# 110 series of products of zeros ahead of the first stage of a hybrid decoder layer

## The chip, the cores and the metric

The kernel runs on one core of a Trainium2 chip. Five engines work side by side, each with a queue of its own that it takes in order: TensorE (PE in the profile, with PEld for the loading of its stationary operand), VectorE (DVE), ScalarE (ACT), GpSimd (POOL) and SyncE (SP), which here only issues DMAs. The metric is the time of one execution on the device in microseconds.

## What is computed

One inference step of one layer, for a prompt of 512 tokens and a sample group of 8 x 8 tokens that share the weights (576 tokens together, width 1024). The layer has three parts, each between two RMS norms:

```python
u = _rms(x) * g_pre_mix
proj = u @ w_in                       # z, xbc, dt, q, k, v, gates, og
...
mix = jnp.concatenate([y_ssd, h_ml], axis=-1) @ w_out
x = x + _rms(mix) * g_post_mix
u = _rms(x) * g_pre_x
qx = (u @ w_xq).reshape(bsz, length, X_HEADS, X_HEAD_DIM)
...
x = x + _rms(o) * g_post_x
u = _rms(x) * g_pre_ffn
f = (jax.nn.silu(u @ w_gate) * (u @ w_up)) @ w_down
x = x + _rms(f) * g_post_ffn
```

The first part mixes a state space scan and an mLSTM scan, the second is attention to a memory of 256 rows, the third a SwiGLU of width 2816. The states and the memory's keys and values are outputs as well.

## The kernel before

The activations lie transposed: 128 features on the partitions, eight feature tiles k, and the 576 tokens in the free dimension. A large product of a weight tile and the tokens is made in fp32r, a reduced form of fp32. To keep the accuracy, both sides are split into a high part and the rest, and three products are summed in one PSUM bank: high weight by high activation, high weight by low activation, low weight by high activation. I call these three a block; a block belongs to one 128 x 128 weight tile and one range of tokens. The helper `gemm` (L200 to L212) does that:

```python
mm(ps, wh, ah, start=i == 0, stop=False)                       # L208
mm(ps, wh, al, start=False, stop=False)                        # L209
m = mm(ps, tiles[order[c]][1], xh(order[c], t0, n), ...)       # L211
```

Each `mm` loads its 128 x 128 stationary operand and streams the moving one. The tokens are cut in two ways: in halves of 256 and 320 (`HALVES`), or of 288 and 288 (`EHALVES`). Eight feature tiles make 24 products in a row for one output tile and one half. The gate, up and down projections run the same three products in `mul` (L1857 to L1859) with 288 columns. The values of the mLSTM (L823) turn the sides round: 128 tokens are the stationary operand, 512 columns of weights move. The memory's values (L803 to L805) do it with 256 columns.

A weight tile arrives as `raw` by a DMA from SyncE's queue; ScalarE casts its high part `whi`, and VectorE subtracts for the low part `wlo` (`split_w`, L177 to L194; in some, GpSimd makes the low part with an adding DMA). These buffers are rings: two `raw`, three `whi`, three `wlo`. Activations and other large things live in slabs of 4608 columns, taken with `SL(slot, ...)`; slot 1 first holds `qk` (L478), whose first write comes after the first tiles of the projection.

PSUM has eight banks. `GP` hands out a ring of three, `MP` another ring of three.

The order of the work: where nothing else is said, the framework's planner puts each engine's instructions into an order, by a simulated time of its own (`schedule_with_timeline_sim`). `tc.issue_after` adds an edge, `tc.high_priority` shifts a part, and `tc.manual_schedule` keeps the written order on the engines named.

The start, around the change: VectorE clears a small tile `wz` (L306), and TensorE multiplies it with itself 21 times into `ps_warm`, a bank of `MP` that nothing reads (L307 to L309). Beside that the parameters, the tokens `xraw` and the first two weight tiles come in (L310 to L339); per feature tile ScalarE makes the high part `uh` and VectorE the low part `ul` of the tokens (L330, L331), and both split the weights. The first products (L347 to L349) follow feature tile by feature tile as these arrive. ScalarE and VectorE sum the squares of the tokens (L274, L275), TensorE sums them over the partitions (L234), and the first stage goes on with `in_tile`, the convolution's tiles (`cb`, L459 to L461) and the gates (`la`, L439).

Of the kernel before, what the change touches and what calls it, by code (L numbers as in the profile page):

```python
# [11 lines left out]
F32 = mybir.dt.float32  # L12
F32R = mybir.dt.float32r
# [6 lines left out]
P = 128  # L20
# [95 lines left out]
def build(nc, tc, ctx, I, O):  # L116
    V, A, G, S, TE = nc.vector, nc.scalar, nc.gpsimd, nc.sync, nc.tensor
    mm = TE.matmul
# [12 lines left out]
    def SL(slot, name, dt=F32, shape=(P, KT, T)):  # L131

        return big.tile(list(shape), dt, name=name, tag="s%d" % slot, bufs=1)
# [5 lines left out]
    def MP(name="m"):  # L139
        return pa.tile([P, 512], F32, name=name, tag="a")  # L140
# [60 lines left out]
    def gemm(ps, units, xh, xl, t0, n, k0=0, k1=None, order=None, late=0):  # L201


        tiles = [(hi[:, j * P:(j + 1) * P], lo[:, j * P:(j + 1) * P]) for hi, lo, nk in units for j in range(nk)]
        order = order or range(len(tiles))
        for i, k in list(enumerate(order))[k0:k1]:
            (wh, wl), ah, al = tiles[k], xh(k, t0, n), xl(k, t0, n)
            mm(ps, wh, ah, start=i == 0, stop=False)  # L208
            mm(ps, wh, al, start=False, stop=False)  # L209
            for c in range(late) if i == late - 1 else [i] if i >= late else ():  # L210
                m = mm(ps, tiles[order[c]][1], xh(order[c], t0, n), start=False, stop=c == len(tiles) - 1)  # L211
        return m  # L212
# [94 lines left out]
    psw = MP("ps_warm")  # L307
    for _ in range(NWARM):
        mm(psw[:, 0:256], wz[:, 0:128], wz, start=True, stop=True, skip_group_check=True)  # L309
    S.dma_start(par, I["par"])  # L310

    wl = [wp.tile([P, 1024], F32R, name="wlo", tag="wlo", bufs=3) for _ in range(2)]
# [3 lines left out]
    for k in range(KT):  # L316
        if k % 2 == 0:
            c = slice(128 * k, 128 * k + 256)
# [42 lines left out]
    stop = gemm(ps0[2][1], [(*w2, KT)], U, UL, 256, 320, 0, NSS)  # L361
# [12 lines left out]
    stop = gemm(ps0[3][0], [(*w3, KT)], U, UL, 0, 256)  # L374
# [343 lines left out]
    for g in range(2):  # L718
        psb = BP("ps_ls")
        pb3 = psb.rearrange("p (h t) -> p h t", h=8)  # L720
        for h in range(8):
            mm(psb[:, h * TS:(h + 1) * TS], sel[:80, 8 * g + h:8 * g + h + 1].to_broadcast([80, P]), cumst[:, TP:T],
               start=h == 0, stop=h == 7, skip_group_check=True)
# [8 lines left out]
        for h in range(8):  # L732
            k, j = h % 2, (8 * g + h) // 2
            mm(psi[64 * k:64 * k + 64, j * TS:(j + 1) * TS], xdts[:, 8 * g + h, :], lm[:, h, :], start=True, stop=True,
               skip_group_check=True)
# [12 lines left out]
    for b in range(4):  # L748
# [3 lines left out]
        for g in range(2):  # L752
            for hb in (1, 0):
# [3 lines left out]
                   start=b == 0, stop=b == 3, skip_group_check=True)  # L757
# [139 lines left out]
    for h in range(4):  # L897
        q, k = qk[:, h, :], qk[:, 4 + h, :]
# [11 lines left out]
        for c in range(4):  # L910
            mm(pss[:, c * P:(c + 1) * P], k[:, c * P:(c + 1) * P], q[:, c * P:(c + 1) * P], start=True, stop=True,
               skip_group_check=True)
# [39 lines left out]
    for h in range(4):  # L952
        mm(psb[:, h * TS:(h + 1) * TS], sel[:68, h:h + 1].to_broadcast([68, P]), sxst[:, TP:T], start=h == 0, stop=h == 3,
           skip_group_check=True)
# [22 lines left out]
    for hb in range(2):  # L977
# [6 lines left out]
        for b in range(4):  # L984
# [3 lines left out]
            for h in range(4):  # L988
                mm(psn[32 * h:32 * h + 32, 0:257], qpad[:, h, bb, :], c0[:, h, 0:257], start=False, stop=b == 3,
                   skip_group_check=True)  # L990
# [242 lines left out]
    x = SL(1, "x1")  # L1233
# [267 lines left out]
    def xo(j, i, pool=None):  # L1501

        t0, n = EHALVES[i]

        with tc.issue_after(evx[j - 3].ins if j > 2 else ovs[5].ins):
            ps, w = GP("ps_xo")[:, :n], weights(("xo", j), I["wxo"][j], pool=pool, cut=1024)

        def step(k0, k1):
            m = gemm(ps, [(*w, KT)], act(oh), act(ol), t0, n, k0, k1, [2, 3, 4, 5, 6, 7, 0, 1], 6 if j == 3 else 0)
            if k1 < KT:  # L1510
                return m
            add_sq(ph, ssq, ps, j if i == 0 else XO1.index(j), n, t0=t0)
            evx.append(A.activation(f[:, j, t0:t0 + n], ps, AF.Copy, scale=PAR("g_postx", j)))
            return m, evx[-1]
        return step
# [10 lines left out]
    for j in range(8):  # L1526
        step = xo(j, 0, wx if 3 < j < 7 else None)
# [21 lines left out]
    W, B = {}, {}  # L1549
# [816 lines left out]
```

## Time and profile before

| | |
|---|---|
| median of the two runs | 1083.56 us (1082.75 to 1084.37) |
| the profiled execution | 1084.31 us |
| its span | 1082.5 us |
| TensorE busy | 1069.4 us, 8124 products recorded |
| VectorE, ScalarE, GpSimd busy | 752.6, 611.0, 226.8 us |
| HBM read and written | 160.28 MB and 20.65 MB |

The span is the time between the first and the last instruction that the profiler recorded. A product's listed duration is not what it costs in a stream: products are pipelined, the next starts before the one before has ended, and the step from start to start is the price. A few per cent of the product records can be missing from a trace. In the timeline a row shows the start, the duration, the engine and line, the operands and the count; in the windows each engine has its busy time and count.

### The profile page before, as it was taken

What the parts mean: (1) busy time and instruction counts of PE and PEld (TensorE: products, weight loads), DVE (VectorE), ACT (ScalarE), POOL (GpSimd) and SP (SyncE); (2) the same over time, 40 slices, a digit from 0 to 9 for tenths busy, and PEclk for the clock granted to TensorE, in tenths of its full rate; (3) what the DMA queues carried; (4) which work ended last, traced back from release to release, by engine and by line L of the source; (5) the groups of instructions that cost most, each with busy time, mean ns of one, the idle gap of its engine ahead of it and who ended that gap; (6) DMA issues with size and microseconds to landing.
All of it is one profiled execution on the core that took longest, in us unless ns stands there. A gap on an engine that the chain in (4) does not pass through costs nothing.

```text
span 1082.5 us, 20708 instructions
## 1 busy us (share of the span) xinstructions
PE 1069.4 (99%) x8124; PEld 1015.6 (94%) x8124; DVE 752.6 (70%) x1507; ACT 611.0 (56%) x1098; POOL 226.8 (21%) x305
## 2 busy tenths in 40 slices
PE   9999999999999999999999999999999999999997
PEld 8999887778999999999999979999999999999997
DVE  6796785748887785558755546766467887787556
ACT  7767532346564556556545545646467566656653
POOL 1342642313122121000144301100011121111000
PEclk9999999999999999999999999999999999999999
DMA  6785635436564439753458775644476687578532
GB/s 207 171 158 121 168 107 190 165 77 189 166 176 124 131 93 331 234 198 103 154 196 291 265 253 185 226 145 96 132 175 143 153 204 168 118 187 187 128 131 89
DMA packets 58966, 182.29 MB, mean 168 GB/s; under 512 B 6604, under 2 KB 11852, under 8 KB 58356
## 3 DMA queue, kind: packets, MB, share of 16 engines
q1 hardware_dynamic: 42740, 138.06, 38.8%
q0 software_dynamic: 15552, 41.95, 19.7%
q8 instruction: 64, 1.05, 0.4%
q10 hardware_dynamic: 576, 0.95, 0.2%
q14 instruction: 34, 0.28, 0.1%
HBM read 160.28 MB, written 20.65 MB: 167 GB/s over the span
## 4 chain that ended last, share of the span: by engine, by line
PE 86%; DVE 5%; ACT 4%; issue 2%; DMA 2%; POOL 0%; DVEq 0%; SPq 0%; ACTq 0%; POOLq 0%
PE ps_in L209 4%; PE ps_in L211 4%; PE ps_in L208 4%; PE ps_v L823 3%; PE ps_o L211 3%; PE ps_g L1858 3%; PE ps_g L1857 3%; PE ps_o L209 3%; PE ps_g L1859 3%; PE ps_o L208 3%; PE ps_u L1858 3%; PE ps_u L1859 3%; PE ps_u L1857 3%; PE ps_dn L1857 2%; PE ps_dn L1858 2%
## 5 line engine op out<-in xcount | busy, mean ns | idle before, releaser
L208 PE MATMUL ps_in<-uh,whi 128*128 128x320 f32 (+1 forms) x544 | 162.5, 299 | 1.5 <-DVE cb L459 0.8
L186 ACT CAST whi<-raw 128x1024 fp32r<-128x1024 f32 (+1 forms) x104 | 105.3, 1014 | 101.3 <-PE ps_in L209 24.7
L211 PE MATMUL ps_in<-uh,wlo 128*128 128x320 f32 (+1 forms) x544 | 162.1, 298 | 0.4 <-DMA wlo<-win 0.4
L209 PE MATMUL ps_in<-ul,whi 128*128 128x320 f32 (+1 forms) x544 | 161.4, 297 | 0.0
L193 DVE TENSOR_TENSOR wlo<-raw,whi 128x512 fp32r<-128x512 f32 (+1 forms) x96 | 94.1, 982 | 77.9 <-ACT whi L186 76.7
L208 PEld LDWEIGHTS ps_in<-uh,whi 128*128 128x128 f32 x544 | 102.3, 188 | 4.8 <-issue 2.3
L211 PEld LDWEIGHTS ps_in<-uh,wlo 128*128 128x128 f32 x544 | 102.3, 188 | 1.6 <-DMA wlo<-win 0.6
L209 PEld LDWEIGHTS ps_in<-ul,whi 128*128 128x128 f32 x544 | 102.4, 188 | 0.6
L191 POOL DMA_DIRECT2D wlo<-win x32 | 27.8, 870 | 80.0 <-ACT wlo L190 72.0
L1857 PE MATMUL ps_g<-b,whi 128*128 128x288 f32 x144 | 42.5, 295 | 0.0
L1858 PE MATMUL ps_g<-b,whi 128*128 128x288 f32 x144 | 42.4, 295 | 0.0
L1858 PE MATMUL ps_u<-b,whi 128*128 128x288 f32 x144 | 42.3, 294 | 0.0
L1857 PE MATMUL ps_u<-b,whi 128*128 128x288 f32 x144 | 42.2, 294 | 0.0
L1830 ACT CAST whi<-rawx 128x1024 fp32r<-128x1024 f32 (+1 forms) x26 | 25.6, 987 | 27.6 <-PE ps_dn L1858 13.7
L198 DVE TENSOR_TENSOR wlo<-sw,whi 128x1024 fp32r<-128x1024 f32 (+1 forms) x26 | 29.6, 1140 | 15.0 <-ACT whi L197 14.9
L208 PE MATMUL ps_xo<-qh,whi 128*128 128x288 f32 x128 | 38.4, 302 | 0.2 <-ACT whi L186 0.2
L209 PE MATMUL ps_xo<-ql,whi 128*128 128x288 f32 x128 | 37.8, 296 | 0.0
L211 PE MATMUL ps_o<-mixm_h,wlo 128*128 128x256 f32 (+1 forms) x128 | 37.7, 295 | 0.0
L209 PE MATMUL ps_o<-mixm_l,whi 128*128 128x256 f32 (+1 forms) x128 | 37.5, 293 | 0.0
L211 PE MATMUL ps_xq<-u2h,wlo 128*128 128x320 f32 (+1 forms) x128 | 37.5, 294 | 0.0
L1809 ACT CAST whi<-raw 128x1024 fp32r<-128x1024 f32 (+1 forms) x26 | 25.6, 984 | 21.1 <-PE ps_g L1858 9.5
L211 PE MATMUL ps_o<-mixs_h,wlo 128*128 128x320 f32 (+1 forms) x128 | 37.5, 293 | 0.0
(769 smaller groups left out, 3847.6 us busy)
## 6 DMA issues: line engine op xcount, KB each, us to landing
raw<-win SPq DMA_DIRECT2D x35, 512.0 KB, 4.1
raw<-wout SPq DMA_DIRECT2D x17, 512.0 KB, 3.8
raw<-wxq SPq DMA_DIRECT2D x13, 512.0 KB, 5.6
raw<-wgate SPq DMA_DIRECT2D x13, 512.0 KB, 3.6
raw<-wup SPq DMA_DIRECT2D x13, 512.0 KB, 5.1
wlo<-win POOLq DMA_DIRECT2D x24, 256.0 KB, 5.2
kva<-vc SPq DMA_DIRECT2D x11, 512.0 KB, 4.9
raw<-wv SPq DMA_DIRECT2D x10, 512.0 KB, 3.9
```

Of the source, the lines that this page charges most:

```text
L186: casts.append(A.copy(hi[:, :n], raw[:, :n]))
L191: G.dma_start(lo[:, a:b], src[:, a:b], accum_op=ALU.add)
L193: e.tensor_tensor(lo[:, a:b], raw[:, a:b], hi[:, a:b].bitcast(F32), op=ALU.subtract)
L198: (eng or V).tensor_tensor(lo, src, hi.bitcast(F32), op=ALU.subtract)
L208: mm(ps, wh, ah, start=i == 0, stop=False)
L209: mm(ps, wh, al, start=False, stop=False)
L211: m = mm(ps, tiles[order[c]][1], xh(order[c], t0, n), start=False, stop=c == len(tiles) - 1)
L823: mm(ps, a, b, skip_group_check=True, **kw)
L1809: s.c1 = A.copy(s.h1[:, s.all], s.r1[:, s.all])
L1857: mm(ps, wh, b[0][k], start=start and k == 0, stop=False, skip_group_check=True)
L1858: mm(ps, wh, b[1][k], start=False, stop=False, skip_group_check=True)
L1859: m = mm(ps, wl, b[0][k], start=False, stop=k == nk - 1, skip_group_check=True)
```

## The change

Behind the 21 warm-up products, and ahead of everything else on TensorE, stands a series of products of zeros. A slab of 4608 fp32r columns, `bench`, is taken from slot 1 and cleared by VectorE. There are 110 strings of six letters. A, B and C are the three products of one block, a, b and c those of the next block: A and C read the same moving operand, B one that lies 1024 columns further; A and B use the same weights, C weights that lie 480 columns further. The first 36 strings are all orders of ABC followed by all orders of abc, the other 74 mix the two blocks. For each string eight segments are written, 12 products in seven of them and 24 in one, with 320, 256, 288 or 512 moving columns; the blocks of a segment advance by 576 columns (one segment: by 288). In the segment of 512 the sides are turned round. All products of the probe go into one bank of `MP`, `ps_probe`, which nothing reads; the first product of a segment clears it. The probe's order is kept as written on TensorE. Nothing else of the kernel is edited; in the changed file the lines behind it stand 22 further.

```diff
     psw = MP("ps_warm")
     for _ in range(NWARM):
         mm(psw[:, 0:256], wz[:, 0:128], wz, start=True, stop=True, skip_group_check=True)
+
+    bench = SL(1, "bench", F32R, (P, 4608))
+    V.memset(bench.bitcast(F32), 0.0)
+    ORDERS = 'ABCabc ABCacb ABCbac ABCbca ABCcab ABCcba ACBabc ACBacb ACBbac ACBbca ACBcab ACBcba BACabc BACacb BACbac BACbca BACcab BACcba BCAabc BCAacb BCAbac BCAbca BCAcab BCAcba CABabc CABacb CABbac CABbca CABcab CABcba CBAabc CBAacb CBAbac CBAbca CBAcab CBAcba BAacCb bCcABa cAbBaC caCABb bAcBCa bCcaBA aCbBcA caAbCB CAbacB cbABaC BcabCA acBACb bBAcaC CcbABa bBAaCc cbBAaC aCAbBc ABcbCa cbBCAa bCcBAa cAabCB BaAbcC aAbCBc aBCbAc cabCBA bCABac cbABCa CBbAac acbABC AbCcaB AbBcCa CbABca CAcaBb cBbCaA abBcCA AcBaCb AbBacC ABabcC AcbaBC CaAcBb cBbACa ACcabB CabBAc aACcBb BCbaAc CabcBA cCbABa BbcAaC abcACB bBcAaC aBcCbA ABaCcb AcCbBa cCABab cBbaAC ACaBcb ACbBca AbBaCc caBbCA CcbAaB bcaACB bBcCaA CcbaBA AaBbCc BCaAcb aCBAbc acABbC BAcabC CaABbc cAbCBa bBcaAC BbACac BCcAba BacbAC'.split()
+    SEG = []
+    for o in ORDERS:
+        SEG += [(o, 320, 576, 256, 12), (o, 256, 576, 0, 12), (o, 320, 576, 256, 12), (o, 256, 576, 0, 12),
+                (o, 288, 576, 0, 12), (o, 288, 576, 32, 12), (o, 288, 288, 0, 24), (o, 512, 576, 0, 12)]
+    pq = MP("ps_probe")
+    with tc.manual_schedule(engines={TE.engine}):
+        for o, n, step, at0, count in SEG:
+            for i in range(count):
+                c = o[i % 6]
+                k = (i // 6 * 2 + (c > "C")) % (4 if step == 576 else 8)
+                c = c.upper()
+                x = 64 + at0 + step * k + (1024 if c == "B" else 0)
+                w = 3600 + (480 if c == "C" else 0)
+                if n == 512:
+                    mm(pq[:, 0:n], bench[:, x:x + P], bench[:, w:w + n], start=i < 1, stop=True, skip_group_check=True)
+                else:
+                    w += 128 * (k % 4)
+                    mm(pq[:, 0:n], bench[:, w:w + P], bench[:, x:x + n], start=i < 1, stop=True, skip_group_check=True)
     S.dma_start(par, I["par"])
 
     wl = [wp.tile([P, 1024], F32R, name="wlo", tag="wlo", bufs=3) for _ in range(2)]
```

## The prediction

> **What bounds the kernel now.** I read the page first (busy shares, clock, chain), then the windows of the first 100 us, then what TensorE waits for, and last the timeline of TensorE alone in four places.
>
> ```profile
> span 1082.5 us, 20708 instructions
> ...
> PE 1069.4 (99%) x8124; PEld 1015.6 (94%) x8124; DVE 752.6 (70%) x1507; ACT 611.0 (56%) x1098; POOL 226.8 (21%) x305
> ...
> PEclk9999999999999999999999999999999999999999
> ...
> q8 instruction: 64, 1.05, 0.4%
> ...
> q14 instruction: 34, 0.28, 0.1%
> ...
> PE 86%; DVE 5%; ACT 4%; issue 2%; DMA 2%; POOL 0%; DVEq 0%; SPq 0%; ACTq 0%; POOLq 0%
> ```
>
> TensorE (PE) is busy for 1069.4 of 1082.5 us at nearly the full granted clock, and the chain that ended last lies on it for 86%. All its idle time is 13.1 us. Whatever is put on TensorE's queue is therefore paid in full, except what fits into those 13.1 us. The profiled execution took 1084.31 us: 1.8 us more than its span, and 0.75 us more than the median of 1083.56.
>
> The change puts products on TensorE, so its price is a number of products times the step from one product to the next. The busy column can't give that step, because products overlap: a 320-column product is listed with 0.30 us, while the next one starts after half of that. I take the step from start times over whole groups of 24 products (8 blocks of three), first rows of neighbouring groups:
>
> ```profile
> 60.75 0.30 PE L208 MATMUL ps_in<-uh,whi 128*128 128x320 f32 x1
> ...
> 64.24 0.28 PE L208 MATMUL ps_in<-uh,whi 128*128 128x256 f32 x1
> ...
> 66.96 0.30 PE L208 MATMUL ps_in<-uh,whi 128*128 128x320 f32 x1
> ...
> 70.46 0.28 PE L208 MATMUL ps_in<-uh,whi 128*128 128x256 f32 x1
> ```
>
> From 60.75 to 64.24 lie 24 products of 320 columns: 3.49 us, 145.4 ns each. From 66.96 to 70.46 lie 24 more: 3.50 us, 145.8 ns each. I take 145.6 ns. Between them, from 64.24 to 66.96, lie 24 products of 256 columns: 2.72 us, 113.3 ns each.
>
> ```profile
> 826.22 0.30 PE L1857 MATMUL ps_g<-u3h,whi 128*128 128x288 f32 x1
> ...
> 829.38 0.29 PE L1857 MATMUL ps_g<-b,whi 128*128 128x288 f32 x1
> ```
>
> 24 steps of 288 columns lie between these two rows: 3.16 us, 131.7 ns each.
>
> ```profile
> 221.81 0.48 PE L823 MATMUL ps_v<-wlo,uh 128*128 128x512 f32 x1
> 222.12 0.40 PE L823 MATMUL ps_v<-whi,uh 128*128 128x512 f32 x1
> ...
> 225.83 0.40 PE L823 MATMUL ps_v<-whi,ul 128*128 128x512 f32 x1
> ```
>
> From 222.12 to 225.83 there are 16 steps of 512 columns: 3.71 us, 231.9 ns each. Here the activations are the stationary side and the weights move, as in the last segment of the change.
>
> **The change, part by part.** Each of the 110 order strings makes eight segments: 12 products of 320 columns, 12 of 256, again 12 and 12 of these, 12 of 288, 12 of 288 shifted by 32 columns, 24 of 288 at a distance of 288, and 12 of 512. That is 24 + 24 + 48 + 12 = 108 products, and 11,880 in all, each with its own weight load (the page has x8124 loads beside x8124 products).
>
> - **The products.** One order costs 24 x 145.6 = 3494 ns, 24 x 113.3 = 2719 ns, 48 x 131.7 = 6322 ns and 12 x 231.9 = 2783 ns, together 15.318 us. Times 110 that is 1685.0 us. All of it is on the path: the probe stands ahead of the first stage in TensorE's queue, every real product stands behind it in the same queue, and a TensorE that runs 99% of the time has nowhere else to put it.
> - **Their weight loads** cost nothing beside that: the groups above hold one load for each product, and their steps contain what the loads cost.
> - **The orders.** The groups above run in one order, hi·hi, lo·hi, hi·lo, block after block. It is one of the 110; the others are not in the trace, so I bound them from both sides. The cheapest column in the quoted groups is that of the 256 group, 113.3 / 256 = 0.4426 ns. An order has 33,792 columns; all of them at that rate make 14.96 us, and 110 orders 1645 us. The dearest long run of 256 columns is this:
>
> ```profile
> L803 PE MATMUL ps_v<-wmh,memhl x16: 283/283/284, 497.8 to 503.2; 128*128 128x256 f32 x16
> ```
>
> L804 and L805 stand between these 16, so 45 steps fill 5.4 us: 120.0 ns each, 1.059 times 113.3. All widths dearer by that factor make 1785 us. This run has its weights in another slab than the weight rings, so other distances between weights and activations; the probe copies those of the ring (its names A, B and C are the three products of a block, at the offsets of the kernel's own tiles). The reordered products read the same places at the same distances, so I take the value of the nearest rows, 1685.0, and keep both ends for the range.
> - **The clock during 1.7 ms of zeros.** The kernel's own warm-up multiplies zeros too:
>
> ```profile
> L309 PE MATMUL ps_warm<-wz x21: 272/421/422, 1.1 to 4.9; 128*128 128x256 bf16 x21
> ...
> 4.65 0.49 PE L309 MATMUL ps_warm<-wz 128*128 128x256 bf16 x3
> ```
>
> Its last three products are two steps apart in 0.49 - 0.27 us, 0.11 us for a step, and the fp32r groups that follow run at the steps above. So zeros keep the clock granted, and I cost the clock at nothing; at half the clock the probe would take twice as long.
> - **The memset.** 4608 columns of one slab on VectorE, right after the memset of the warm-up's tile:
>
> ```profile
> 0.84 0.17 DVE L306 MEMSET wz<- 128x128 uint32 x1 [0.84 <-PEq L2358]
> ...
> 5.48 0.39 PE L347 MATMUL ps_in<-uh,whi 128*128 128x256 f32 x1 [0.34 <-ACT whi L197]
> ...
> L198 DVE TENSOR_TENSOR wlo<-sw,whi 128x1024 fp32r<-128x1024 f32 x18 | 22.0, 1223 | 14.9 <-ACT whi L197 14.9
> ```
>
> It starts at about 1.0 and takes at least the 0.17 of the small one and at most 4.5 x 1.223 = 5.5 us, so it ends between 1.2 and 6.5. The warm-up ends at 4.65 + 0.49 = 5.14. The probe thus waits 0 to 1.4 us; I take 0.5, a start at 5.6, where the first real product started at 5.48: +0.1 us. What is queued behind the memset on VectorE are the first low halves (`ul`, `wlo`), and only products behind the probe wait for these: 1685 us of cover.
> - **The inputs.** The DMA queues and ScalarE go on during the probe until the rings are full (two `raw`, three `whi`, three `wlo`), so at its end the first tiles lie ready. What that can save is TensorE's early waiting:
>
> ```profile
> 5.00:20.00 15.00, 14.66 (x111) 14.38 (x110) 11.27 (x21) 10.96 (x21) 0.96 (x3) 1.00 0.91 311
> 20.00:40.00 20.00, 18.47 (x140) 17.42 (x139) 15.02 (x29) 13.14 (x20) 5.92 (x19) 1.00 0.43 117
> ...
> PE ps_ss L234 <- DVE ssqx L275: 1.2, 1, 1.2
> ...
> PE ps_in L208 <- DVE cb L459: 0.8, 1, 0.8
> ```
>
> The first windows idle 0.34 and 1.53 us. The sums of squares (1.2 us) need only the inputs and are done during the probe; `cb` is made from TensorE's own results, so its wait and those like it stay. I take 1.2 + 0.3 = 1.5 us off, with 13.1 us (all idle time) as the most that can go. On the dear side the planner, which orders each queue by a simulated time, may now order the first stages otherwise; another 13 us is the bound I set there, the idle time once more.
> - **Instructions.** (1.05 + 0.28) MB for 20,708 instructions is 64 bytes each; 23,760 more make 1.5 MB. TensorE takes one pair in 15.318 / 108 = 142 ns in the probe, and takes one in 131.7 ns in the 288 group without a gap, so I cost the fetch at nothing. The DMA engines, which have little to do once the rings are full, cover it; without that cover the price would be gaps between products.
> - **Places.** The zero slab shares its slot with `qk`, first written long after the probe. The probe's PSUM bank is one of the ring of three; it is free when its last product ends, and TensorE's next users come later in the same queue. Both cost nothing.
>
> Sum, against the profiled execution: 1084.3 + 1685.0 + 0.1 - 1.5 = 2767.9 us, rounded to 2768.
>
> **The rivals.**
> - *The plain stream rate.* The fp32r steps hold more than the columns need, and this part may come from traffic that is absent in the probe or from the kernel's order. For it speaks the warm-up: 0.109 us for 256 columns (0.11 above), 0.426 ns for a column. Against it: in the quoted 256 group the steps stay at 113.3 as an average of 24, and in the 320 and 288 groups at even more a column, in places of quite different load. It would give 33,792 x 0.426 x 110 = 1583 us, so 2666.
>
> The Trainium skill, "TensorE: Matmul & The Clock Gate", section "Back-to-back issue gap", gives a warm gap of N / 2.4 + 2.5 ns. By it an order takes 14.35 us, the probe about 1579 us and the kernel about 2661, as an estimate from that page. This case's trace does not follow it for fp32r: 113.3, 131.7, 145.6 and 231.9 ns stand against 109.2, 122.5, 135.8 and 215.8.
> - *Dear orders.* If mixing two blocks brings the worse distances of L803 into most orders, all products cost 1.059 times as much: 1785 us, so 2867. The 120.0 ns speak for it, the copied distances against it.
> - *Weight loads that show.* If a load can no longer run beside the product ahead of it, the step grows; the step from 221.81 to 222.12 is 0.31 in place of 0.232. At one product in six this is 1980 x 0.08 = 158 us: 2926. Against it: every product has a new load already, and PEld is busy 94% of the span beside PE.
> - *Not slower.* Nothing reads the probe's bank, so something on the way may drop its products, or they may lie in idle time. Then the time stays at 1084. The warm-up's bank is not read either, and its 21 products are all in the row of L309; the idle time holds 13.1 us at most. It decides only if fewer than 150 products remain (2% is 21.7 us, at 142 ns each).
>
> **How the numbers follow.** The forecast has 0.85, the plain rate 0.05, dear orders 0.05, loads that show 0.03, not slower 0.01, and something unforeseen 0.01. The range begins at the cheap end of the forecast, 1084.3 + 1645 - 1.4 = 2728, and ends where half the products are dear, 1685 + 50, so 2818; the 13 us of the planner lie inside. What lies outside has about 0.15. A measurement of this kernel can tell about 2% from no change: slower by more than that 0.985, within it 0.01, faster 0.005.
>
> **What the profile after would show.** Some 20,000 products in place of 8124, 10,560 of them on the added line for 256 to 320 columns and 1,320 on that for 512; a clock of nines throughout; VectorE, ScalarE and DMA nearly empty from about 20 us to 1690 us; then the old picture. The groups' first starts should lie 24 x 0.1456 us and so on apart. A first real product before 1650 or after 1740 us would say that the steps were wrong; a remainder behind the probe longer or shorter than 1077 us by more than 13 us, that the side effects were.

## The result and the profile after

The changed kernel takes 2772.35 us (median of two runs, 2771.82 and 2772.87), against 1083.56 before: 2.5565 times as long, with an interval of 2.5518 to 2.5611. The forecast was 2768. First the page of the changed kernel, the lines that answer to those of before:

```profile
span 2771.1 us, 44473 instructions
...
PE 2758.5 (100%) x20004; PEld 2648.3 (96%) x20004; DVE 755.5 (27%) x1508; ACT 611.3 (22%) x1098; POOL 226.9 (8%) x305
...
PEclk9999999999999999999999999999999999999999
DMA  2000000000000000000000001654647466657773
...
q8 instruction: 156, 2.56, 0.4%
...
PE 95%; DVE 2%; ACT 1%; DMA 1%; issue 1%; POOL 0%; DVEq 0%; ACTq 0%; POOLq 0%; SPq 0%
PE ps_probe L331 50%; PE ps_probe L328 11%; PE ps_in L209 2%; PE ps_in L208 2%; PE ps_in L211 2%; PE ps_v L845 1%; PE ps_o L211 1%; PE ps_g L1880 1%; PE ps_g L1879 1%; PE ps_o L209 1%; PE ps_g L1881 1%; PE ps_o L208 1%; PE ps_u L1880 1%; PE ps_u L1881 1%; PE ps_u L1879 1%
```

Exactly 11,880 products were added, and the other engines' busy times are within 3 us of those before. In 23 of the 40 slices the DMA engines are busy for less than a tenth, while TensorE works on at the full granted clock. The probe's two lines make 61% of the chain. Its edges, and the memset ahead of it, in the timeline:

```profile
1.91 3.90 DVE L312 MEMSET bench<- 128x4608 f32 x1 [0.91 <-issue]
...
5.74 0.69 PE L369 MATMUL ps_in<-uh,whi 128*128 128x256 f32 x3 [0.52 <-ACT whi L197]
6.26 12.69 PE L331 MATMUL ps_probe<-bench 128*128 128x320 f32 x96
...
1693.69 2.94 PE L328 MATMUL ps_probe<-bench 128*128 128x512 f32 x12
1696.47 0.28 PE L370 MATMUL ps_in<-ul,whi 128*128 128x256 f32 x1
```

The probe lasts from 6.26 to 1696.47, 1690.2 us, where the sum had 1685.0. Three real products slipped in ahead of it. What lies around the probe is 2771.1 - 1690.2 = 1080.9 us, against the old span of 1082.5. To see where those 1.6 us came from, the same two products in the kernel before and in the changed one:

```profile
85.08 0.31 PE L211 MATMUL ps_in<-uh,wlo 128*128 128x320 f32 x1
...
1075.09 0.30 PE L2200 MATMUL ps_ft<-c,sw 128*128 128x128 f32 x1
```

```profile
1772.32 0.31 PE L211 MATMUL ps_in<-uh,wlo 128*128 128x320 f32 x1
...
2763.65 0.31 PE L2222 MATMUL ps_ft<-c,sw 128*128 128x128 f32 x1
```

The distance is 1687.24 us at the first pair and 1688.56 at the last. The probe took 1690.2 us and the first product started 0.26 us later than before; less 1687.24 that is 3.2 us won up to the first pair. Behind it 1.3 us are lost again. TensorE's waits in the changed kernel name some of the places:

```profile
PE ps_os L1430 <- DMA kva<-vc: 1.0, 2, 0.7
PE ps_in L208 <- DVE cb L481: 0.8, 1, 0.8
...
PE ps_os L1430 <- ACT kva L1455: 0.4, 1, 0.4
```

The wait of 1.2 us for the sums of squares is gone, the 0.8 for `cb` is still there, and 1.4 us at L1430, for the sample group's cached keys and values, is new.

### The profile page after: what moved, and what is told of

Its sections match the earlier page's. It is cut to its first block, busy times and chain, and to the rows that moved or that the text cites. A ratio compares the mean times of both kernels' runs of the same rounds, so it can differ in the third digit from the quotient of the medians.

```text
span 2771.1 us, 44473 instructions
## 1 busy us (share of the span) xinstructions
PE 2758.5 (100%) x20004; PEld 2648.3 (96%) x20004; DVE 755.5 (27%) x1508; ACT 611.3 (22%) x1098; POOL 226.9 (8%) x305
## 4 chain that ended last, share of the span: by engine, by line
PE 95%; DVE 2%; ACT 1%; DMA 1%; issue 1%; POOL 0%; DVEq 0%; ACTq 0%; POOLq 0%; SPq 0%
PE ps_probe L331 50%; PE ps_probe L328 11%; PE ps_in L209 2%; PE ps_in L208 2%; PE ps_in L211 2%; PE ps_v L845 1%; PE ps_o L211 1%; PE ps_g L1880 1%; PE ps_g L1879 1%; PE ps_o L209 1%; PE ps_g L1881 1%; PE ps_o L208 1%; PE ps_u L1880 1%; PE ps_u L1881 1%; PE ps_u L1879 1%
## 5 line engine op out<-in xcount | busy, mean ns | idle before, releaser
L331 PEld LDWEIGHTS ps_probe<-bench 128*128 128x128 f32 x10560 | 1397.3, 188 | 9.5
L331 PE MATMUL ps_probe<-bench 128*128 128x288 f32 (+2 forms) x10560 | 1403.0, 294 | 0.0
L328 PE MATMUL ps_probe<-bench 128*128 128x512 f32 x1320 | 322.8, 393 | 0.0
L328 PEld LDWEIGHTS ps_probe<-bench 128*128 128x128 f32 x1320 | 241.9, 188 | 47.6
L186 ACT CAST whi<-raw 128x1024 fp32r<-128x1024 f32 (+1 forms) x104 | 105.4, 1014 | 104.9 <-PE ps_in L209 31.4
```

The costliest lines, as they stand in the source:

```text
L186: casts.append(A.copy(hi[:, :n], raw[:, :n]))
L328: mm(pq[:, 0:n], bench[:, x:x + P], bench[:, w:w + n], start=i < 1, stop=True, skip_group_check=True)
L331: mm(pq[:, 0:n], bench[:, w:w + P], bench[:, x:x + n], start=i < 1, stop=True, skip_group_check=True)
```

## The experiments

The steps below are the mean differences of neighbouring start times in the trace, by the width of the first of the two, over all products of the probe (ns). "Rest" is the span less the probe.

| kernel | 256 | 288 | 320 | 512 | probe, us | rest, us |
|---|---|---|---|---|---|---|
| the prediction's rows | 113.3 | 131.7 | 145.6 | 231.9 | 1685.0 | |
| changed kernel | 115.05 | 131.93 | 145.79 | 231.07 | 1690.2 | 1080.9 |
| e1, one order | 114.65 | 131.61 | 145.46 | 231.67 | 1687.4 | 1079.7 |
| e2, dearest order | 118.39 | 132.16 | 146.59 | 231.38 | 1702.8 | 1079.2 |
| e3, bf16 | 109.17 | 122.5 | 135.86 | 215.67 | 1578.4 | 1081.3 |
| e4, dear distance | 119.80 | 132.52 | 146.56 | 229.22 | 1705.5 | 1084.1 |
| e7, data | 115.22 | 131.93 | 146.35 | 231.07 | 1692.2 | 1088.1 |
| e8, one product | 116.04 | 132.64 | 146.59 | 229.17 | 1696.2 | 1088.9 |
| e9, only 256 | 113.34 | | | | 1346.4 | 1081.8 |

In e3 some records of 512 columns are missing, so its 288 is worked out from the total: (1578.4 - 2.640 x 109.17 - 2.640 x 135.86 - 1.320 x 215.67) / 5.280. The steps from one product of 288 columns to the next, which no missing record touches, give 122.50 too. The rest of e7 includes 6.6 us by which its probe starts later.

**e1 and e2: one order alone.**

```diff
-    ORDERS = 'ABCabc ABCacb ...'.split()
+    ORDERS = ['ABCabc'] * 110        # e1
+    ORDERS = ['aAbCBc'] * 110        # e2
```

> All 110 strings are ABCabc, the kernel's own order. Theory (the step belongs to width, operand type and order, and the quoted groups of the kernel are this order): one order takes 15.311 us as its single instance did in the changed kernel, so 1684.2 us of probe in place of 1690.2 and 2766.4 us in all. Rival (the orders' differences in one instance are chance): no difference, 2772.

> All 110 strings are aAbCBc, the dearest order of the changed kernel (15.480 us in its one instance). Theory (the order fixes the step): 1702.8 us of probe, 2785.0 us. Rival (chance): 2772.

Measured: 2772.48 us (2768.91 to 2775.79) and 2786.43 us (2783.75 to 2788.63). These medians are less sharp than the question, since the rest varies (the four executions of e1 alone lie 6.9 us apart); the probe's edges in the timeline, first of e1 and then of e2, settle it.

```profile
6.17 12.74 PE L331 MATMUL ps_probe<-bench 128*128 128x320 f32 x96
...
1693.59 0.28 PE L370 MATMUL ps_in<-ul,whi 128*128 128x256 f32 x1
```

```profile
6.16 12.82 PE L331 MATMUL ps_probe<-bench 128*128 128x320 f32 x96
...
1708.91 0.28 PE L370 MATMUL ps_in<-ul,whi 128*128 128x256 f32 x1
```

The dearest order takes 1702.8 us, as forecast: its differences in one instance were no chance. The kernel's order takes 1687.4 us, between the two expectations. Step by step the reason is seen. These are the steps of the two 256 segments in e1, in ns, the same within 1 ns in all repetitions:

```
behind 320 columns:  117 123 118 115 120 118 114 113 113 114 113 113
behind 320 columns:  113 114 113 113 114 113 113 114 113 113 114 113
```

The same twelve products, at the same addresses, cost 116.0 ns in one segment and 113.3 in the other. Only what ran before differs: the first of them comes behind the 320 segment that follows the 512 one. In this order a step depends on the products before it and settles after some seven. In aAbCBc it does not come down: both 256 segments of e2 hold 118.4 ns.

**e9: only 256 columns.** All strings are ABCabc here too.

```diff
-        SEG += [(o, 320, 576, 256, 12), (o, 256, 576, 0, 12), ...]
+        SEG += [(o, 256, 576, 0, 12)] * 9
```

> All strings ABCabc, and all nine segments of 12 are of 256 columns (108 products, as before). In the one-order run the 256 segment behind one of 320 began at 117 to 123 ns and fell to 113.3 within seven products, the next one stayed at 113.3. Theory (a step depends on what ran before it, and settles): all at 113.33 ns, 1346.4 us of probe and 2428 to 2430 us. Rival (the mean of the mixture, 114.65 ns, is the price of the order): 1362 us of probe, 2444 us.

Measured: 2429.96 us (2429.58 to 2435.94). The timeline's edges:

```profile
6.32 15.27 PE L330 MATMUL ps_probe<-bench 128*128 128x256 f32 x133
...
1352.75 0.28 PE L369 MATMUL ps_in<-ul,whi 128*128 128x256 f32 x1
```

1346.4 us for 11,880 products is 113.3 ns each. With no other width between them the 256 products stay at the settled step, so the 114.65 of e1 belong to the mixture. For this order the theory of a settling step holds.

**e3: bf16.**

```diff
-    bench = SL(1, "bench", F32R, (P, 4608))
-    V.memset(bench.bitcast(F32), 0.0)
+    bench = SL(1, "bench", BF16, (P, 4608))
+    V.memset(bench, 0.0)
```

> The same orders with a bf16 slab of zeros, so that the same column offsets are half as many bytes apart. Theory (the part of the step above the plain stream rate belongs to the 4-byte operands, as the warm-up's 0.109 us for 256 bf16 columns says): about 0.426 ns a column, 1583 us of probe, 2665 us; by the rule of the Trainium skill, TensorE: Matmul & The Clock Gate, section Back-to-back issue gap, an estimate of 1579 us of probe and 2661 us. Rival (it belongs to the orders, to the weight loads or to the traffic beside): 2772.

Measured: 2661.77 us (2660.35 to 2664.29). The edges in the timeline, and the weight loads of the 512 products among the instructions of L328, first of the changed kernel and then of e3:

```profile
6.64 11.98 PE L331 MATMUL ps_probe<-bench 128*128 128x320 bf16 x96
...
1585.01 0.47 PE L370 MATMUL ps_in<-ul,whi 128*128 128x256 f32 x1
```

```profile
L328 PEld LDWEIGHTS ps_probe<-bench x1320: 187/188/192, 18.7 to 1696.0; 128*128 128x128 f32 x189
...
L328 PEld LDWEIGHTS <-bench x1320: 97/98/98, 18.3 to 1584.8; 128*128 128x128 bf16 x189
```

In bf16, with the same orders and columns, the probe takes 1578.4 us. So the plain rate exists, and the 112 us above it belong to the operand type, fp32r in place of bf16, and not to the orders or the traffic beside, which are the same. Whether the four bytes or another trait of fp32r is behind it was not tested. A weight load's record is 98 ns in bf16 and 188 in fp32r; whether the surplus comes from the loads or from the moving operand's reads, this run doesn't part. The distances in bytes were halved as well; the run in which the weights were moved (e4) shows 15 us, not 112.

The Trainium skill's rule for the gap of an isolated product, N / 2.4 + 2.5 ns ("TensorE: Matmul & The Clock Gate", section "Back-to-back issue gap"), meets the bf16 steps of this stream to 0.2 ns at all four widths; on the fp32r steps it is 5.9 to 15.2 ns too low.

**e4: the dear distance.**

```diff
-                w = 3600 + (480 if c == "C" else 0)
+                w = 3520 + (512 if c == "C" else 0)
```

> The weights moved from column 3600 to 3520 and the C weights to 512 columns behind the A weights in place of 480, so that weights and moving operand lie a multiple of 256 bytes apart, as in the memory's values (120.0 ns for 256 columns). Theory (this distance dears the 256 products alone, since the 256 step is near the length of a weight load): 256 columns at about 119.5 ns, the others as before, plus 12 us, 2784 us. Rival (it dears every width by 1.059): about 2870. Rival (distances do nothing): 2772.

Measured: 2787.84 us (2786.79 to 2791.32). The edges:

```profile
6.25 12.93 PE L331 MATMUL ps_probe<-bench 128*128 128x320 f32 x96
...
1711.71 0.28 PE L370 MATMUL ps_in<-ul,whi 128*128 128x256 f32 x1
```

The probe grows by 15.3 us. The 256 products go to 119.80 ns, as in the memory's values, and bring 12.5 of it (2640 x 4.75). That the place of the weights matters is shown; the edit moved their first column and the distance of the C weights together, and which of the two did it is not. That it matters for 256 columns alone was too simple, since 288 and 320 rose by 0.6 and 0.8 ns and 512 fell by 1.9. A factor of 1.059 on every width is excluded. Why 256 suffers most stays open: the expectation's reason, a step near the length of a weight load, isn't what the records show, 188 ns for an fp32r load and 113 to 120 for the step.

**e8: the same product six times.**

```diff
-    ORDERS = 'ABCabc ABCacb ...'.split()
+    ORDERS = ['AAAAAA'] * 110
```

> All strings are AAAAAA: every second block, six times the same moving operand and the same weights in a row. Theory (the step above the bf16 rate belongs to reading 4-byte operands, and the order only shifts it by a per cent): 1670 to 1700 us of probe, 2752 to 2782 us. Rival (it comes from going to another place with each product): the bf16 steps, 1578 us of probe, 2661 us. Rival (a load of the same weights is left out or cheaper): less still in the 256 products, which are near the load's own length.

Measured: 2781.72 us (2779.16 to 2786.89). The edges, and TensorE's longest waits:

```profile
6.29 12.82 PE L331 MATMUL ps_probe<-bench 128*128 128x320 f32 x96
...
1702.48 0.28 PE L370 MATMUL ps_in<-ul,whi 128*128 128x256 f32 x1
```

```profile
PE ps_os L1430 <- ACT kva L1455: 3.3, 1, 3.3
PE ps_os L1430 <- DMA kva<-vc: 1.7, 2, 1.0
PE ps_o L208 <- ACT f_mix L1115: 1.2, 2, 0.9
```

1696.2 us: going to no other place saves nothing, and weights that were just loaded are loaded again at no lower price. The surplus is not the price of moving about. The waits tell another thing: this kernel's instructions stand in the same order on every engine as the changed kernel's, and yet its rest is 8 us longer, mainly in waits for `kva` and `f_mix` that the changed kernel has shorter or not at all. Behind two of the waits for `kva`, the granted clock (the third figure from the right) was halved for 3.4 us:

```profile
2332.40:2335.70 3.30, 3.30 (x13) 1.60 (x12) 0.00 (x0) 0.00 (x0) 0.00 (x0) 0.50 0.94 380
```

The four executions of e8 alone lie 7.7 us apart, and the profiled one is the longest of them. The rest is uncertain by that much. Seven kernels have this same order on every engine: the changed one, e1 to e4, e8 and e9. In all seven the product that started at 85.08 us before comes 2.3 to 3.2 us earlier than 85.08 us and the probe together. What they lose behind it ranges from nothing to 9.3 us. So the early gain repeats, and the later loss does not.

**e7: data in place of zeros.**

```diff
-    V.memset(bench.bitcast(F32), 0.0)
+    S.dma_start(xs, I["xT"])
+    V.tensor_copy(bench.rearrange("p (k t) -> p k t", t=T), xs)
```

> The slab holds the tokens in place of zeros (a DMA into the slab of xs, and a copy by VectorE in place of the memset), so the probe multiplies data. Theory (the step doesn't depend on the values): probe of 1690.2 us, begun some 8 us later because it waits for the DMA and the copy, 2780 us. Rival (zeros are cheap, data lower the clock or lengthen the steps): a longer probe and a granted clock below 0.99.

Measured: 2781.76 us (2780.52 to 2782.53), granted clock 0.999.

```profile
12.22 0.85 PE L370 MATMUL ps_in<-uh,whi 128*128 128x256 f32 x2 [6.50 <-ACT whi L197]
12.87 14.64 PE L332 MATMUL ps_probe<-bench 128*128 128x320 f32 x96
...
1705.02 0.28 PE L371 MATMUL ps_in<-ul,whi 128*128 128x256 f32 x1
```

The probe starts 6.6 us later and takes 1692.2 us, 2 us more, which lie at its beginning: its first row of 96 products takes 14.64 us in place of 12.69, behind a TensorE that had idled for 6.5 us. The first steps, in ns:

```
320 columns:  314 267 266 267 267 266 267 267 266 267 267 266
256 columns:  214 213 213 214 122 116 119 123 118 115 120 118
```

These are steps at half the clock. The trace of e5 below has a granted clock of 0.50 from 80.4 to 83.8 us, and there 320 columns of the kernel's own products take 267 ns too, just behind it 146. The first warm-up products of the changed kernel take 213 ns for 256 columns of bf16. So at half the clock the fp32r surplus isn't there, and a step at half the clock is 1.8 to 1.9 times one at the full clock and not twice. A mean of 0.999 doesn't show such a beginning. These 24 products hold all of the 1.9 us; from the 25th on every step is that of the zeros within 1 ns. The values don't set the step.

**e5 and e6: no products, and a tenth of them.**

```diff
-    for o in ORDERS:
+    for o in ():                     # e5
+    for o in ORDERS[:11]:            # e6
```

> The slab and its memset stay, the 11,880 products go. Theory (all but a microsecond of the change is the products' steps): the memset delays the first real product by 0.26 us as in the changed kernel, so the time of the kernel before plus 0.3. Rival (the slab, the bank or the planner's order cost or save microseconds of their own): off by 2 us or more.

> Only the first 11 of the 110 strings. In the changed kernel these took 169.1 us. Theory (price proportional to the products, and once for all about 1.6 us less for the rest of the kernel, as 2771.1 less 1690.2 of probe stands to 1082.5): the kernel before plus 167.5. Rival (a fixed price at the start or end of the probe, or a rate that sinks in a long probe): more than 3 us off.

Measured: e5 1083.04 us against 1084.22 of the kernel before beside it, a ratio of 0.9983 (0.9972 to 0.9993); e6 1254.5 us, 170.3 above.

```profile
5.91 12.76 PE L331 MATMUL ps_probe<-bench 128*128 128x320 f32 x96
...
175.08 0.28 PE L370 MATMUL ps_in<-ul,whi 128*128 128x256 f32 x1
```

The eleven orders of e6 take 169.2 us, as the first eleven of the 110 did, so the price is proportional; its total is 2.8 us above the expectation, all of it in the rest (1084.1). The median of e5 is 1.2 us below the kernel before, where +0.3 was expected; that is less than the rival's 2 us off. TensorE's list of waits in e5 begins so:

```profile
PE ps_ct L584 <- ACT r L563: 1.2, 1, 1.2
PE ps_warm L309 <- DVE wz L306: 1.1, 1, 1.1
```

The wait of 1.2 us for the sums of squares is gone here as well, with no probe to make time for them; so is that of 0.8 for `cb`. The memset and the slab alone give the planner other simulated times, and it writes another order on TensorE, VectorE, ScalarE, GpSimd and SyncE. The changed kernel's order differs as well, both from that of the kernel before and from that of e5. The product after the sums, first before and then in e5:

```profile
25.85 0.40 PE L208 MATMUL ps_in<-uh,whi 128*128 128x320 f32 x1
```

```profile
24.86 0.39 PE L208 MATMUL ps_in<-uh,whi 128*128 128x320 f32 x1
```

It starts 1.0 us earlier. The product that started at 60.07 us before comes 1.8 us earlier in e5, and 2.3 in the changed kernel, less the probe. So most of this gain needs no probe, and what the inputs that lie ready add to it can't be told apart from the planner's order. At the product that started at 85.08 us before, the profiled execution of e5 has 0.2 us of it left; between the two stand the 1.2 us at L584 and a stretch at half the clock:

```profile
80.00:84.00 4.00, 4.00 (x18) 3.81 (x18) 3.90 (x7) 3.90 (x7) 2.14 (x5) 0.57 0.79 183
```

## Why the prediction was right, point by point

- *The products.* Right to 0.3%: 1690.2 for 1685.0 us. The 5.2 us are the term of the steps: 256 columns 2640 x 1.75 ns = 4.6, 288 columns 5280 x 0.23 = 1.2, 320 columns 0.5, and 512 columns -1.1. The group from which 113.3 was read was a settled one; behind other widths and in other orders the mean step is 113 to 118 ns (e1, e2).
- *The orders.* Bounded rightly. Over the 110 strings an order takes 15.298 to 15.480 us, 1.2% apart, and the kernel's own, at 15.311 in its one instance, is among the cheapest.
- *The weight loads, the clock of zeros, the instructions.* All three at nothing, and so it came: the steps contain the loads (PEld x20004), the granted clock stayed full and data ran at the same steps (e7), and q8 grew by 1.51 MB without a gap. That half the clock would have doubled the probe was a little too much: e7's first steps are 1.8 to 1.9 times the full ones.
- *The memset.* 3.90 us, from 1.91 to 5.81, within its bounds. The probe began at 6.26 and not at 5.6, but three real products used that time; the first of them came 0.26 us late in place of 0.1. That is not the memset's doing: the product waited for `whi`, and in e5, with the same memset, it started at 5.38, 0.1 us earlier than before. No run shows a price of the memset.
- *The inputs.* The size came out by luck, and the reason isn't borne out. 3.2 us went in the first stages where 1.5 were forecast, and 1.3 came back, mostly at L1430; behind the first pair, kernels in the same order lost from nothing (e2) to 9.3 us (e8). The step that isn't borne out is the one that counted on the full rings, since e5 shows most of the early gain without the probe. The planner's order, which the prediction had as a bound of 13 us and not as a term, was at work; how much of the 3.2 us is its share stays open.
- *The rivals.* The plain rate was a true rate of the wrong operand type (e3). Dear orders and a dear place of the weights exist, at 1% of the probe and not at 5.9% (e2, e4). Loads that show, and products that vanish, did not occur.

The profiled execution took 2772.87 us, 5.0 above the sum of 2767.9: 5.2 from the steps, and 0.2 back from the rest (1080.9 - 1082.5 = -1.6, for +0.1 - 1.5).

## What to carry to other kernels

On an engine that is busy all the time, added work costs its count times its step; read the step from start times over a whole group, not from the busy column, and for the same operand type. A group read in one place is a settled one: other orders, neighbours and places moved the whole probe here by 1% and 256 columns alone by up to 6% (113.3 to 119.8 ns). Don't explain microseconds around such a block by readiness before a run without the block has shown that the planner hasn't simply written another order.

## What the runs showed of the hardware

- At the full granted clock, the step of an fp32r product is above that of bf16 at every width: 113.3 to 109.2 ns at 256 columns, 131.9 to 122.5 at 288, 145.8 to 135.9 at 320, 231.1 to 215.7 at 512.
- At half the clock it is not: 213 ns for 256 columns of either type (the warm-up, e7), and 267 for 320 columns of fp32r (e5, e7).
- The fp32r step is exact and has a memory: the same twelve products took 116.0 or 113.3 ns each, by what ran a dozen products earlier, and repeated within a nanosecond a hundred times (e1).
- Two programs with the same order of instructions on every engine differed by 8 us outside the probe (1080.9 and 1088.9), mainly in waits for the cached keys and values and for `f_mix`; the longer one also had a granted clock of 0.50 for 3.4 us (e8).
